# A two-layer hybrid attention trunk on one core: the memory's keys and values become the first chunk of weights, and bank reads of norms and values move ahead of weight work

## The chip, the cores and the metric

The kernel runs on one core of a Trainium2 chip. The metric is the time of one execution in device microseconds (us), median over runs. The engines are TensorE (PE: matmuls and transposes, which write to the banks of PSUM), VectorE (DVE), ScalarE (ACT), GpSimd (POOL) and SyncE (SP). Each takes its own instructions in the order in which the program wrote them. SP issues most of the DMAs, POOL some.

## The reference

Two layers on 512 tokens of width 1024. Layer 0 mixes by dilated windows, layer 1 by grouped queries; both also attend, with four heads, to 256 memory tokens. Cut to what the change touches:

```
for i in range(DEPTH):
    h = rmsnorm(x, norm_g[i])
    mem_h = rmsnorm(mem, mem_norm_g[i])
    proj = einsum('bsd,de->bse', h, w_in[i])
    ...
    kv = einsum('bnd,de->bne', mem_h, w_mem_kv[i]).reshape(B, 256, 2, 4, 128)
    k = rmsnorm(kv[:, :, 0], mem_kn_g[i])
    v = kv[:, :, 1]
    ...
    x = x + einsum('bse,ed->bsd', y * silu(gate), w_out[i])
```

All is float32. The keys and values of the memory don't depend on x, so they may be worked out before or after the first projection of the layer.

## The kernel before

**Precision.** Each float32 operand is split in a high part (a rounded copy, made on ACT) and a low part (what is left, made on DVE), and a product is three matmuls: high x high, high x low, low x high (`mm3`, L162 to L165). Of weights these parts are the tiles `wh` (ACT, L285) and `wo` (DVE, L295); of x the tiles `h`, `hS` (turned by PE at L471, copied by ACT at L157, low part by DVE at L160), of the memory `act`.

**Chunks.** The weights lie in DRAM as pieces of 128x1024 (512 KB), in the order of `PLAN`; the work on them is cut into chunks. A chunk of kind `W2` or `W1` (`s_chunk`, L352) multiplies two 2x2 block matrices with seven products in place of eight, in which sums of weight blocks (`T1` to `T4`) and sums of x blocks (`S1` to `S4`, made from `xs` at L506 to L516) stand for blocks. A chunk of kind `T2`, `T2b` or `O1` (`chunk`, L331) is a plain product. The first three chunks of before are one `W2` (the values of head group 0, from x; 14 pieces of 12 matmuls), and two `T2` (the memory's keys and values; 4 pieces each, again 12 matmuls a piece, `mem_kv` at L593). After them comes the memory's queries, a `W1` chunk.

**What sets the order.** Nothing is scheduled by a planner: the order of an engine's instructions is that in which the Python code emits them. `Driver` keeps generators with due times, counted in slots; a slot is one piece of a `W` chunk or one group of a `T2` chunk. After a group's matmuls come, in this order: `drv.free()` (generators given to `release`, which read banks), `W.advance()` (low parts, weight sums, casts, loads), and `drv.tick()` (generators given to `spawn`). `W.advance` casts a piece ahead of its use, into a ring of four `wh`/`wo` buffers (`RING`, L24); a cast whose buffer is still read waits on its engine and holds what is behind it. `KEEP` (L38) limits how many loaded pieces are held per kind.

**The start.** The gain of the layer's norm is spread over the partitions by one-row matmuls into two banks (`row_bank`, L557); two rows of dummy matmuls (`busy`, L884) keep PE at work. Two of four x tiles are normed (`norm_1`: squares on ACT, the root on POOL; `norm_2`: DVE) and turned, then the first `W2` product begins, while `prep` (L857) norms the other two, makes the sums and turns them. The memory's norm (`mem_norm(0)`) is spawned five slots later, and its keys and values follow after the `W2` chunk. Layer 1 uses the same `mem_kv` and `chunk`, with its first part (`mem_norm(1)`) spawned in layer 0's output projection.

**The evacuations.** `chunk` spawns what follows a bank two slots after its last group, so behind the weight work of that slot. `ev_k` (L597) squares the keys per head, multiplies by the root, turns them, and splits them into `kmT`; `ev_v` (L606) splits the values into `vm`.

Of the kernel before, what the change touches and what calls it, by code (L numbers as in the profile page):

```python
# [24 lines left out]
XW, BOTH = (1, 2, 0, 5), False  # L25
BULK, ACTIVE, MEM_AT, SET_AT, WARM, MEM_B, PREP_Y, ACC_AT, PREP_B, HALF, SET_B = 2, 2, 5, 15, 1, 12, 1, 4, 1, {"a": 3, "b": 3, "o": 0}, 3
MEM_STEP = 1, 1
MEM_D = 4
PD, W_EARLY = 1, True
# [95 lines left out]
def trunk_kernel(ctx: ExitStack, tc: tile.TileContext, x, mem, wall, norm_g, mem_norm_g, gcol,  # L125
# [50 lines left out]

    class Weights:
        def __init__(self):
            self.items, self.last, self.need, self.allocs, self.sums = [], [], [], [], []
            self.users = {}  # L180
            d = g = 0
            for c, kind in enumerate(PLAN):
# [12 lines left out]
                else:  # L195
                    n = 1 if kind in ("W1", "W1b") else 2
                    at = {k: d + i * n for i, k in enumerate(("21", "11", "12", "22"))}
                    d += 4 * n
# [11 lines left out]
            assert d == wall.shape[0], (d, wall.shape)  # L210
# [27 lines left out]
        def sum(self, force=False, want=None):  # L238

            for n, (key, d) in enumerate(self.sums[:8]):  # L240
# [12 lines left out]
                elif k == "T2":  # L253
                    if not (self.ripe(self.load_at, key, force) and self.ripe(self.at, (c, "T1", x), force, 1 if c < T1_DMA else None)):
                        continue
                    if c:
                        G.dma_start(self.tile[key], self.tile[c, "T1", x], accum_op=ALU.add)
                    else:
                        V.tensor_tensor(self.tile[key], self.tile[key], self.tile[c, "T1", x], ALU.add)
# [16 lines left out]
        def hi(self, force=False):  # L276
            i = self.n_hi
            if i >= len(self.items) or not self.ripe(self.at, self.items[i], force, 1 if self.items[i][1] == "T1" and self.items[i][0] < T1_DMA or self.items[i][:2] == (0, "T2") else None):
                return False
# [51 lines left out]
    def chunk(units, nb, group, evac):  # L331

        ps = [None] * nb
        for u in range(units):
# [150 lines left out]
    def proj_t(act, sels, evac):  # L485
# [5 lines left out]
        chunk(2, len(sels), group, evac)  # L491
# [65 lines left out]
    def row_bank(name, times=1):  # L557

        r = [at("row") for _ in range(2)]
# [33 lines left out]
    def mem_kv(layer, M):  # L593
# [249 lines left out]
    for c, n in enumerate(XW):  # L843
        nc.sync.dma_start(xt[c], xv[c])
        W.dma(n)
# [670 lines left out]
```

## Time and profile before

| | |
|---|---|
| median of 3 runs | 972.06 us (971.13 to 972.48) |
| the profiled execution | 971.6 us |
| its span, first to last instruction | 969.8 us |
| PE busy | 949.5 us |
| DVE busy | 793.1 us |
| ACT busy | 675.4 us |
| first weight matmul starts | 9.65 us |
| query chunk starts (after the first three chunks) | 86.32 us |
| mean granted TensorE clock | 1.000 |

The profile is of one execution. Its timeline gives each instruction's start and duration in us, the engine, the line, the operation, and output and inputs by the program's names with the buffer numbers left out; in brackets stands the idle time before it and what ended it. "x8" merges eight equal instructions that follow each other. A view of waits lists who waited for whom, with the total in us, the number of waits and the longest. A view of stretches gives each engine's busy time between two points of the span, with the granted clock, the share of DMA and its GB/s. Instructions overlap their predecessor's drain, so the distance between two starts is shorter than a duration.

### The profile page before, as it was taken

The page shows a single profiled execution, that of the slowest core. Times are in us where ns is not written, and L with a number is a line of the kernel's source. Part 1 is how long each engine was busy: PE and PEld are TensorE (multiplying, and loading weights), DVE is VectorE, ACT ScalarE, POOL GpSimd, SP SyncE. Part 2 cuts the span into 40 slices and gives each one's busy share as a digit, 9 for nine tenths or more (in the row PEclk, how much of TensorE's full clock was granted, in tenths as well). Part 3 has the DMA queues.
Part 4 walks back from the last instruction along what each step waited for, and adds up shares of the span by engine and source line. Part 5 has one row for each costly group of instructions (what it writes and reads, how often), then busy time and mean ns, then how long its engine had stood idle before and what let it go on. Part 6 is the DMA issues. An engine that isn't in the chain of part 4 may idle for free. (4 is left out here: it accounts for less than half of the span.)

```text
span 969.8 us, 16665 instructions
## 1 busy us (share of the span) xinstructions
PE 949.5 (98%) x5728; PEld 835.8 (86%) x5728; DVE 793.1 (82%) x1413; ACT 675.4 (70%) x1687; POOL 332.7 (34%) x480
## 2 busy tenths in 40 slices
PE   8899999999999999999999999999999999999998
PEld 5689988888888888888899996787999999998776
DVE  6997776888888888888898999769888997779863
ACT  6555689686868686868685667545778887878760
POOL 1122423556454545454736011323233231011011
PEclk9999999999999999999999999999999999999999
DMA  8979846968787868685959889959986696786644
GB/s 331 326 267 336 220 102 170 293 131 259 150 256 154 256 153 261 154 260 131 279 134 233 259 203 272 299 191 351 240 178 148 178 241 166 218 213 163 183 140 130
DMA packets 88982, 209.27 MB, mean 216 GB/s; under 512 B 25281, under 2 KB 36033, under 8 KB 88898
## 3 DMA queue, kind: packets, MB, share of 16 engines
q1 hardware_dynamic: 70034, 146.28, 43.5%
q0 software_dynamic: 17568, 59.78, 32.5%
q10 hardware_dynamic: 1296, 2.16, 0.6%
q8 instruction: 45, 0.74, 0.3%
q14 instruction: 39, 0.32, 0.1%
HBM read 157.79 MB, written 12.65 MB: 176 GB/s over the span
## 5 line engine op out<-in xcount | busy, mean ns | idle before, releaser
L295 DVE TENSOR_TENSOR wo<-wl,wh 128x1024 fp32r<-128x1024 f32 x255 | 314.6, 1237 | 12.3 <-ACT wh L285 11.5
L285 ACT CAST wh<-wl 128x1024 fp32r<-128x1024 f32 x255 | 269.7, 1059 | 75.7 <-PE pj L165 39.8
L163 PE MATMUL pj<-wh,hS 128*128 128x512 f32 (+1 forms) x448 | 164.3, 367 | 0.0
L164 PE MATMUL pj<-wo,hS 128*128 128x512 f32 (+1 forms) x448 | 158.1, 353 | 2.6 <-DVE wo L295 2.6
L165 PE MATMUL pj<-wh,hS 128*128 128x512 f32 (+1 forms) x448 | 158.2, 353 | 0.0
L163 PE MATMUL pj<-wh,h 128*128 128x512 f32 (+1 forms) x336 | 123.4, 367 | 0.0
L164 PE MATMUL pj<-wo,h 128*128 128x512 f32 (+1 forms) x336 | 118.8, 354 | 2.3 <-DVE wo L295 2.3
L165 PE MATMUL pj<-wh,h 128*128 128x512 f32 (+1 forms) x336 | 118.9, 354 | 0.0
L420 POOL TENSOR_TENSOR rstd<-mse,half 128x4 f32<-128x4 f32 (+2 forms) x98 | 100.1, 1021 | 8.2
L164 PEld LDWEIGHTS pj<-wo,hS 128*128 128x128 f32 x448 | 85.0, 190 | 13.4 <-DVE wo L295 3.5
L165 PEld LDWEIGHTS pj<-wh,hS 128*128 128x128 f32 x448 | 84.7, 189 | 12.4 <-DVE hS L160 0.3
L163 PEld LDWEIGHTS pj<-wh,hS 128*128 128x128 f32 x448 | 84.8, 189 | 9.7
L419 POOL TENSOR_SCALAR mse<-hss 128x4 f32<-128x4 f32 (+1 forms) x86 | 44.3, 515 | 129.9 <-ACT junk L529 126.1
L360 ACT COPY sn<-pj 128x512 f32<-128x512 f32 x132 | 73.6, 591 | 14.3 <-PE pj L165 10.7
L529 ACT ACTIVATE junk<-sn 128x128 f32<-128x128 f32 x264 | 79.0, 308 | 0.2 <-DVE sn L371 0.2
L987 POOL TENSOR_TENSOR ta<-sn,tabs 128x128 f32<-128x128 f32 (+1 forms) x64 | 37.2, 584 | 119.7 <-DVE sn L534 91.6
L164 PEld LDWEIGHTS pj<-wo,h 128*128 128x128 f32 x336 | 64.0, 190 | 10.0 <-DVE wo L295 2.8
L165 PEld LDWEIGHTS pj<-wh,h 128*128 128x128 f32 x336 | 63.7, 190 | 9.3 <-DVE h L160 0.2
L163 PEld LDWEIGHTS pj<-wh,h 128*128 128x128 f32 x336 | 63.9, 190 | 7.3 <-ACT h L157 0.2
L377 DVE TENSOR_TENSOR sn<-pj,sn 128x512 f32<-128x512 f32 x99 | 67.5, 683 | 3.0 <-PE pj L165 2.6
L269 POOL DMA_DIRECT2D wl<-wl x33 | 29.3, 886 | 112.4 <-DVE wo L295 70.7
L163 PE MATMUL pj<-hS,wh 128*128 128x256 f32 x192 | 55.9, 291 | 0.0
(229 smaller groups left out, 2457.1 us busy)
## 6 DMA issues: line engine op xcount, KB each, us to landing
wl<-in_wall_dram SPq DMA_DIRECT2D x222, 512.0 KB, 6.9
wl<-wl POOLq DMA_DIRECT2D x64, 512.0 KB, 5.8
wl<-in_wall_dram POOLq DMA_DIRECT2D x42, 512.0 KB, 8.5
acc<-sn POOLq DMA_DIRECT2D x16, 256.0 KB, 5.0
od<-o SPq DMA_DIRECT2D x12, 256.0 KB, 5.2
og<-od SPq DMA_DIRECT2D x12, 256.0 KB, 6.8
odb<-o SPq DMA_DIRECT2D x12, 256.0 KB, 2.7
og<-odb SPq DMA_DIRECT2D x12, 256.0 KB, 3.9
```

The source lines that it names most:

```text
L163: T.matmul(o, lh, rh, start=start, stop=False, skip_group_check=True)
L164: T.matmul(o, lh, rl, start=False, stop=False, skip_group_check=True)
L165: T.matmul(o, ll, rh, start=False, stop=stop, skip_group_check=True)
L269: G.dma_start(self.tile[key], self.tile[c, "T2", x], accum_op=ALU.add)
L285: A.copy(wh, self.tile[self.items[i]])
L295: V.tensor_tensor(wo, self.tile[key], wh.bitcast(F32), ALU.subtract)
L360: A.copy(t, b)
L377: V.tensor_tensor(t, b, t, ALU.subtract if q == "12" else ALU.add)
L419: G.tensor_scalar(e, ss, EPS, None, ALU.add)
L420: G.tensor_tensor(r, e, half[:, 0:n], ALU.pow)
L529: A.activation(jk, p[:, j * 128:(j + 1) * 128], AF.Square, scale=QS, accum_out=ss[:, j:j + 1])
L987: G.tensor_tensor(ta[:, 0:n], xn[:, 0:n, 0:32], ropeA[:, 0, b, s0:s0 + n], ALU.mult)
```

## The change

The order of the first chunks is no longer that of `PLAN` (in which the weights still lie in DRAM) but `SEQ`: the two `T2` chunks first, then the `W2`. So the memory tiles and the gain of their norm are loaded and normed ahead of x; the gain of x goes by banks to an SBUF tile (`gain`, copied by ACT in `ahead`); the four x tiles are loaded and normed behind them in `prep`, the x parts turned while the memory's chunk runs. `ahead` turns the memory's tiles just ahead of the groups that use them. The T2 sums of the first `W2` chunk go by DMA. The mask and rope tables are loaded in `setup`. In `chunk`, used by both layers and by the output projections, the evacuation goes to `release` and stands ahead of `W.advance`; `ev_k` gives what follows its squares to `release`, too, and `ev_v` makes its low part at once.

```diff
-KEEP = {"T2": 6, "T2b": 4, "O1": 4, "W1": 9, "W2": 10, "W2s": 9, "W1b": 7, "W2b": 9}
+SEQ = [1, 2, 0] + list(range(3, len(PLAN)))
+KEEP = {"T2": 8, "T2b": 4, "O1": 4, "W1": 9, "W2": 10, "W2s": 9, "W1b": 7, "W2b": 9}
...
-            for c, kind in enumerate(PLAN):
+            for c in SEQ:
+                kind, d = PLAN[c], sum(pieces(k) for k in PLAN[:c])
...
-                    if c:
-                        G.dma_start(self.tile[key], self.tile[c, "T1", x], accum_op=ALU.add)
-                    else:
-                        V.tensor_tensor(self.tile[key], self.tile[key], self.tile[c, "T1", x], ALU.add)
+                    G.dma_start(self.tile[key], self.tile[c, "T1", x], accum_op=ALU.add)
...
+                if pre:
+                    pre(u, b)
                 group(w, u, b, ps[b])
                 drv.free()
+                if u == units - 1:
+                    drv.release(evac(b, ps[b]), 2)
                 W.advance()
-                if u == units - 1:
-                    drv.spawn(evac(b, ps[b]), 2)
                 drv.tick()
...
         def ev_k(b, p):
             r = head_sq(p)
-            yield 2
-            xn = head_mul(p, r)
-            yield 2
-            q = transpose4(xn)
...
+            def rest():
+                xn = head_mul(p, r)
+                yield 2
+                q = transpose4(xn)
+                cs = slice(b * 128, (b + 1) * 128)
+                yield from put_norm(q, gk_m[layer], kt_[0][:, :, cs], kt_[1][:, :, cs])
+            drv.release(rest(), 2)
+            yield 1
...
             A.activation(vt_[0][:, b], p, AF.Copy, scale=0.5)
-            yield 1
             V.scalar_tensor_tensor(vt_[1][:, b], p, 0.5, vt_[0][:, b].bitcast(F32), ALU.mult, ALU.subtract)
+            yield 1
...
-    nc.sync.dma_start(row0, norm_g[0:1, :])
-    rows["x0"] = halves(row0)
-    for c, n in enumerate(XW):
-        nc.sync.dma_start(xt[c], xv[c])
-        W.dma(n)
+    nc.sync.dma_start(row0, mem_norm_g[0:1, :])
+    rows["m0"] = halves(row0)
+    row1 = m4(name="row1")[0:1, :]
+    nc.sync.dma_start(row1, norm_g[0:1, :])
+    rows["x0"] = halves(row1)
+    for b in range(2):
+        nc.sync.dma_start(mt[b], mem[b * 128:(b + 1) * 128])
+        W.dma(1)
+    W.dma(2)
...
+    for c in range(4):
+        nc.sync.dma_start(xt[c], xv[c])
+        if c % 2:
+            W.dma(2)
...
+        for c in range(5):
+            if c < 4:
+                n[c] = norm_1(xb[c])
+            if c:
+                norm_2(xb[c - 1], n[c - 1], rows["x"])
+                if c > 2:
+                    s1.append(sum_h(xb[c - 1]))
+            if 1 < c < 4:
+                put_h(H, "12", c - 2, xb[c - 2][1])
+                put_h(H, "11", c - 2, xb[c - 2][0])
             yield 1
         for c in range(2):
             sums_h(H, xb[c], xb[2 + c], c, s1[c], sums)
-            yield 1
+            yield 2 - c
...
-    first = row_bank("x0", WARM)
+    first = row_bank("m0", WARM)
+    gain = row_bank("x0", 1, pj)
...
-    busy(512)
-    nst[0] = norm_1(xb[0], True)
+    nst = [norm_1(mb[0], True)]
     W.hi(True)
-    norm_2(xb[0], nst[0], first, (1,))
+    norm_2(mb[0], nst[0], first, (0,))
...
+    def ahead(u, b):
+        if (u, b) == (0, 1):
+            for j in range(2):
+                A.copy(rows["x"][j], gain[j])
+            norm_3(mb[1], M, 128, 0)
+            for c in range(2):
+                norm_2(mb[c], nst[c], first, (1,))
+        if (u, b) == (1, 0):
+            for c in range(2):
+                norm_3(mb[c], M, 128 * c, 1)
...
-    drv.spawn(mem_norm(0), MEM_AT)
-    s_chunk(512, H, ev_v0, pre=second)
-    km, vm = mem_kv(0, Ms[0])
+    km, vm = mem_kv(0, M, ahead)
+    s_chunk(512, H, ev_v0)
```

Three places show how the order of instructions moves. The first is ACT's queue at the point where x is first turned (`sq` are the squares of a norm, `junk` those of a key's heads, `h` is x turned, `act` the memory turned). Before, the casts of `h` stand between the first two weight pieces:

```order
L458 ACTIVATE sq,ss<-x 128x512 x2
L157 CAST h_134<-xT 128x4x128
L285 CAST wh<-wl 128x1024
L157 CAST h_134<-xT 128x4x128
L157 CAST h_179<-xT 128x4x128
```

With the change, after the second 24 matmuls of the key chunk:

```order
L462 ACTIVATE sq,ss<-x 128x512 x2
L533 ACTIVATE junk,hss<-pj 128x128 x4
L287 CAST wh<-wl 128x1024 x2
L462 ACTIVATE sq,ss<-x 128x512 x2
L158 CAST h_341<-xT 128x4x128
L158 CAST h_349<-xT 128x4x128
```

The first casts of x now stand behind the seventh and eighth weight pieces (`x2`) and behind the squares of the third x tile.

The second place is DVE's queue around the x sums of the `W2` chunk. Before (`xs_257` to `xs_314`, the second x half's sums; L251 and L259 are weight sums):

```order
L506 TENSOR_TENSOR xs_257<-x 128x512
L295 TENSOR_TENSOR wo<-wl,wh 128x1024
L251 TENSOR_TENSOR wl<-wl 128x1024
L160 TENSOR_TENSOR hS_286<-xT,hS_286 128x4x128
L514 TENSOR_TENSOR xs_284<-xs_235,x 128x512
L515 TENSOR_TENSOR x<-x 128x512
L516 TENSOR_TENSOR xs_285<-x,xs_284 128x512
L295 TENSOR_TENSOR wo<-wl,wh 128x1024
L259 TENSOR_TENSOR wl<-wl 128x1024
L160 TENSOR_TENSOR hS_286<-xT,hS_286 128x4x128
L514 TENSOR_TENSOR xs_314<-xs_257,x 128x512
```

With the change (`xs_446` takes the place of `xs_257`, `xs_534` that of `xs_314`):

```order
L510 TENSOR_TENSOR xs_446<-x 128x512
L297 TENSOR_TENSOR wo<-wl,wh 128x1024 x2
L161 TENSOR_TENSOR hS_465<-xT,hS_465 128x4x128
L518 TENSOR_TENSOR xs_463<-xs_406,x 128x512
L519 TENSOR_TENSOR x<-x 128x512
L520 TENSOR_TENSOR xs_464<-x,xs_463 128x512
L617 SCALAR_TENSOR_TENSOR vm<-pj,vm 128x512
L594 SCALAR_TENSOR_TENSOR kmT<-qT,gc,kmT 128x4x128
L617 SCALAR_TENSOR_TENSOR vm<-pj,vm 128x512
L297 TENSOR_TENSOR wo<-wl,wh 128x1024 x2
L594 SCALAR_TENSOR_TENSOR kmT<-qT,gc,kmT 128x4x128
L161 TENSOR_TENSOR hS_465<-xT,hS_465 128x4x128
```

The row that follows is `xs_534`. The values (`vm`), the keys (`kmT`) and two more weight pieces stand ahead of it. PE turns it right after the second `W2` piece.

The third place is DVE's queue at the start of layer 1, where the same `mem_kv` runs (`tabs` are its rope tables, `xn` is a key's norm, reading the bank `pj`). Before:

```order
L1225 TENSOR_TENSOR tabs<-tbraw,grB 128x512
L534 TENSOR_TENSOR xn<-pj,rstd 128x512
L295 TENSOR_TENSOR wo<-wl,wh 128x1024 x2
L160 TENSOR_TENSOR hS_8035<-xT,hS_8035 128x4x128
L514 TENSOR_TENSOR xs_8066<-xs_7998,acc 128x512
```

With the change:

```order
L1248 TENSOR_TENSOR tabs<-tbraw,grB 128x512
L538 TENSOR_TENSOR xn<-pj,rstd 128x512
L297 TENSOR_TENSOR wo<-wl,wh 128x1024 x2
L1248 TENSOR_TENSOR tabs<-tbraw,grB 128x512
L510 TENSOR_TENSOR xs_8019<-acc 128x512
L538 TENSOR_TENSOR xn<-pj,rstd 128x512
L161 TENSOR_TENSOR hS_8044<-xT,hS_8044 128x4x128
```

Both key norms are now done before the first S1 low part (`hS`), a pair of weight pieces sooner than before.

More of the change, by code (lines that the diff above doesn't have):

```diff
@@ L209, in __init__ @@
                             g += 1
-            assert d == wall.shape[0], (d, wall.shape)
+            assert sum(pieces(k) for k in PLAN) == wall.shape[0]
             self.g = -1
@@ L555, in row_load, with row_bank @@
         rows[name] = halves(t)
-    def row_bank(name, times=1):
-        r = [at("row") for _ in range(2)]
+    def row_bank(name, times=1, bank=at):
+        r = [bank("row") for _ in range(2)]
         for j in (1, 0):
@@ L838, in trunk_kernel @@
     rows = {}
+    mt = [m4(name="m") for _ in range(2)]
     nc.scalar.dma_start(ident, ident_d)
     row0 = m4(name="row0")[0:1, :]
[L841 to L845 removed]
+    nc.sync.dma_start(row0, mem_norm_g[0:1, :])
[7 more added lines that the diff above has]
+    W.dma(2)
     tabA = s2(name="tabA")[:, 0:256].rearrange("p (b c d) -> p b c d", b=2, c=4)
@@ L880, in setup @@
             yield 1
-    first = row_bank("x0", WARM)
+    first = row_bank("m0", WARM)
+    gain = row_bank("x0", 1, pj)
+    rows["x"] = halves(m4(name="row"))
     def busy(n):
-        T.matmul(at("busy")[:, 0:n], ones, rows["x0"][0][0:1, 0:n], start=True, stop=True)
-    busy(512)
-    nst[0] = norm_1(xb[0], True)
+        T.matmul(at("busy")[:, 0:n], ones, rows["m0"][0][0:1, 0:n], start=True, stop=True)
+    mb, M = [halves(t) for t in mt], Act(NM)
+    nst = [norm_1(mb[0], True)]
     W.hi(True)
-    norm_2(xb[0], nst[0], first, (1,))
+    norm_2(mb[0], nst[0], first, (0,))
     def mid():
```

63 lines of the change are left out of this document (23 added, 40 removed).

## The prediction

> **What bounds the kernel now.** I read the page's busy shares first, then the waits of TensorE (PE), then the busy time in stretches, to see which stage has room for the change.
>
> ```profile
> PE 949.5 (98%) x5728; PEld 835.8 (86%) x5728; DVE 793.1 (82%) x1413; ACT 675.4 (70%) x1687; POOL 332.7 (34%) x480
> ...
> PE pj L164 <- DVE wo L295: 6.7, 8, 2.0
> ...
> PE pj L164 <- DVE wo L295: 4.6, 4, 2.0
> PE xT L471 <- DVE h L160: 0.8, 1, 0.8
> ...
> 10.00:16.00 6.00, 5.18 (x21) 4.13 (x21) 4.30 (x7) 3.07 (x8) 0.40 (x2) 1.00 1.02 410
> 16.00:46.00 30.00, 25.42 (x129) 20.25 (x127) 28.53 (x36) 16.95 (x27) 6.01 (x10) 1.00 0.99 317
> 46.00:72.00 26.00, 26.00 (x126) 21.73 (x125) 23.88 (x32) 16.42 (x27) 5.19 (x9) 1.00 0.76 277
> 72.00:110.00 38.00, 38.00 (x255) 35.08 (x254) 26.55 (x26) 22.63 (x54) 12.46 (x15) 1.00 0.95 290
> ```
>
> PE is busy 98% of the span, so the whole is set by matmul work, and no matmul of weight is added or removed. Over the run PE waits 6.7 us for low parts of weights (`wo`, made on VectorE, DVE); the second row of that name is the first 50 us alone: 4.6 of the 6.7. In the stretches (columns PE, PEld, DVE, ACT, POOL) DVE is busy 28.5 of 30 us from 16 to 46 while PE is not full; from 46 on PE is full. So the only place to win or lose more than a microsecond is the first 46 us, and there DVE ends last. The question is whether the new order has DVE ready earlier or later than PE needs it.
>
> **The start of PE.** These rows of the timeline give start, duration, engine and line.
>
> ```profile
> 2.24 3.75 PE L562 MATMUL row<-row,ones 1*128 1x512 f32 x4 [2.24 <-DMA row<-in_norm_g_dram]
> 5.78 1.91 PE L886 MATMUL busy<-row,ones 1*128 1x512 f32 x2
> 7.87 1.11 PE L471 MATMUL xT<-ident,x 128*128 128x128 f32 x4 [0.17 <-DVE x L465]
> 9.02 0.58 ACT L157 CAST h<-xT 128x512 fp32r<-128x512 f32 x1
> 9.65 0.80 PE L163 MATMUL pj<-wh,h 128*128 128x512 f32 x1
> ...
> 10.68 0.63 PE L165 MATMUL pj<-wh,h 128*128 128x512 f32 x1
> 11.10 0.63 PE L163 MATMUL pj<-wh,h 128*128 128x512 f32 x1
> ...
> 15.57 0.39 PE L164 MATMUL pj<-wo,h 128*128 128x512 f32 x1
> 15.80 0.39 PE L165 MATMUL pj<-wh,h 128*128 128x512 f32 x1
> ```
>
> Three one-row products (two `row`, one `busy`) keep PE until 7.69; each costs 1.7 us plus 0.2 of drain (1.91). The change has four, since the gain of x gets banks too and `busy(512)` goes: PE is free for the first transposes at about 7.69 + 1.7 - 0.2 = 9.2. The norm of the first memory tile, some 0.4 us later than that of x now because one more row is loaded ahead of it, is done by 8.2 and not the last. From transposes to the first matmul it takes 9.65 - 7.87 = 1.78, so that matmul starts at 11.0: 1.3 us later than now.
>
> Matmuls step by 0.42 us at 11.10 and by 0.23 at 15.57: PE is at half speed until somewhere before 15.57. The granted-clock column says 1.00 throughout, so I go by the steps. I assume full speed from 15.0 here too: (15.0 - 11.0)/0.42 = 9.5 slow matmuls and 2.5 at 0.23 end the first twelve at 15.6. Bounds: full speed from 13 saves 0.9; from 18 it costs 1.5.
>
> [...]
>
> **Sizes.** The next rows are from the timeline of before, PE, ACT and DVE apart.
>
> ```profile
> 83.70 0.39 PE L165 MATMUL pj<-wh,act 128*128 128x512 f32 x1
> ...
> 85.74 0.39 PE L165 MATMUL pj<-wh,act 128*128 128x512 f32 x1
> 85.97 0.60 PE L541 MATMUL qT<-ident,xn 128*128 128x128 f32 x4
> 86.32 0.36 PE L163 MATMUL pj<-wh,h 128*128 128x256 f32 x1
> ...
> 37.56 1.03 PE L471 MATMUL xT<-ident,xs 128*128 128x128 f32 x8
> 38.20 1.07 ACT L157 CAST hS<-xT 128x512 fp32r<-128x512 f32 x2
> 41.59 1.03 PE L471 MATMUL xT<-ident,x 128*128 128x128 f32 x8
> 45.21 1.03 PE L471 MATMUL xT<-ident,x 128*128 128x128 f32 x8
> ...
> 36.10 2.00 ACT L285 CAST wh<-wl 128x1024 fp32r<-128x1024 f32 x2 [1.97 <-DVE wl L259]
> 17.20 0.63 ACT L458 ACTIVATE sq<-x 128x512 f32<-128x512 f32 x1
> 18.44 1.05 ACT L285 CAST wh<-wl 128x1024 fp32r<-128x1024 f32 x1
> ...
> 662.46 1.41 DVE L465 SCALAR_TENSOR_TENSOR acc<-acc,rstd,row 128x512 f32<-128x512 f32 x2
> 663.78 0.22 DVE L1222 TENSOR_SCALAR grB<-grB 128x128 f32<-128x128 f32 x1
> 665.85 2.35 DVE L295 TENSOR_TENSOR wo<-wl,wh 128x1024 fp32r<-128x1024 f32 x2
> 668.12 0.68 DVE L506 TENSOR_TENSOR xs<-acc 128x512 f32<-128x512 f32 x1
> 668.72 0.68 DVE L1225 TENSOR_TENSOR tabs<-tbraw,grB 128x512 f32<-128x512 f32 x1
> 680.47 0.74 DVE L590 SCALAR_TENSOR_TENSOR kmT<-qT,gc,kmT 128x512 fp32r<-128x512 f32 x1
> 681.13 1.27 DVE L160 TENSOR_TENSOR hS<-xT,hS 128x512 fp32r<-128x512 f32 x2
> ```
>
> Starts are what counts where DVE runs without a break: a 512-wide operation 0.60 (668.12 to 668.72), a pair of norms 1.32 (662.46 to 663.78), two low parts 2.27 (665.85 to 668.12; a weight sum has the same shape), a key's low part 0.66. A warm matmul is 2.04/9 = 0.227 (83.70 to 85.74, ten rows), twelve 2.72; twelve with eight transposes 3.62 (41.59 to 45.21), so four transposes 0.45. A cast follows its transposes' start by 0.64 (37.56 to 38.20) and takes 0.55.
>
> **The key chunk.** After the first twelve the second memory tile is turned and used at once: 15.6 + 0.64 + 0.55 = 16.8, its low part (0.6) by 17.45, the third matmul then, ten more matmuls 2.27: 19.7. The two second halves are turned next: cast by 20.9, but DVE has a pair of norms and two low parts first (17.4 + 1.32 + 2.27 = 21.0), so the low part is there at 21.65; ten matmuls give 24.0, twelve more 26.7. That ends 48 matmuls. Now comes the in-order wait I rest most on. ACT's casts of weight pieces 7 and 8 need ring buffers that PE reads until 26.7, and behind them on ACT stand the squares of x tile 2 and the casts of the first turned x: 26.85 + 1.95 + 1.24 (17.20 to 18.44) + 0.55 = 30.6. DVE, done with the norm of x tile 1 at about 27.2, waits 3.4 us for those casts, because the x low parts stand ahead of its weights.
>
> **The vector engine's run.** From 30.6 to the sum `xs_534` DVE has, without a break, four low parts of turned x, two key norms, two first sums, two S1 low parts, four later sums and two values' low parts (16 x 0.60 = 9.6), two key low parts (1.3), six weight low parts and two weight sums (8 x 1.135 = 9.1), two pairs of norms (2.6): 22.7, ending at 53.3. PE's own work up to that sum, counted from 26.7, is six groups of twelve matmuls and nine blocks of four transposes: 26.7 + 6 x 2.72 + 9 x 0.45 = 47.1. DVE is 6.2 us behind that, and PE meets it in three places. `xs_406`, the first sum, is 7.1 us into the run: 37.7 against 36.7, a wait of 1.0. The low part of the first `W2` piece follows 6.0 later: 43.7 against 42.0, a wait of 1.7. And `xs_534` comes at 53.3 against 49.8, since two later weights, the values and a key stand ahead of it: 3.5. What PE has left then is 12 x 12 matmuls and seven blocks: 12 x 2.72 + 7 x 0.45 = 35.8, so the query chunk begins at 89.1. Now it begins at 86.32 with one block (0.45) still to do, so 86.8 is its like. That is 2.3 us late; six hand-overs between engines at the 0.05 seen from 9.60 to 9.65 add 0.3: **2.6 us**. Behind `xs_534` DVE's load per piece is one low part and two 0.60 operations, 2.3 us against PE's 2.72 to 3.62, so I expect no further wait.
>
> The bounds of this term: by PE's work alone it would be 2.6 - 6.2 = -3.6; if DVE lost another 0.1 us at each of the run's 30 operations, +5.6.
>
> **What costs nothing.** The T2 sums of the first wide chunk leave DVE (2.27 us) for two DMAs on POOL's queue:
>
> ```profile
> wl<-wl POOLq DMA_DIRECT2D x2, 512.0 KB, 7.8
> ...
> 657.65 1.42 DVE L465 SCALAR_TENSOR_TENSOR acc<-acc,rstd,row 128x512 f32<-128x512 f32 x2 [1.45 <-DMA x1d<-acc]
> ...
> PE qT L541 <- DVE xn L534: 0.3, 1, 0.3
> ```
>
> They can start once the second T1 sum is there, at about 41, and land 7.8 us later; PE wants the pieces past 65, so they are hidden. Without that cover the 7.8 us would show. On POOL's queue the two table products of the set-up now stand between these DMAs and the last T4 sums, in the query chunk instead of the value chunk; the T4 pieces are wanted some 20 us after their sources, so 0, and a few us if POOL's order held them. The mask, table and gain loads leave SP's queue near 11 us for slot 15, inside the `W2` chunk: five weight loads pass them, and the first head needs them only after the query chunk. The broadcast load of the memory's gain (512 KB) disappears; DMA isn't the bound, so 0. In layer 1 the earlier key norms stand ahead of two low parts (0.6 later), while the 0.3 wait of qT goes and the accumulator sums come a slot earlier, ahead of a norm that waits 1.45 now for a DMA of them: bounds -1.1 to +0.6, taken as 0.
>
> Sum: 971.6 (the profiled execution; span 969.8 and 1.8 around it) + 2.6 = 974.2. The median of the runs shown is 0.5 above that execution: **974.7 us**. Clock and hand-over bounds put the likeliest case's own range at 973 to 978.
>
> **Rivals.** (1) *DVE isn't late*: if the x casts get through ACT before the weights' buffers are free, or the run is shorter, the 6.2 us of waits go and PE's late start alone is left: 974.7 - 6.2 = 968.5. For it: weight sums and T1/T2 work of DVE fall by 2.27 us, and the value chunk has pieces without sums. Against: the queue is in order and the 3.4 us idle stands ahead of everything. It decides when DVE resumes by 24.4 instead of 30.6; halfway there the time is within 0.2%. (2) *A weight piece is late*: the first T1 load is the 19th big transfer; at 410 GB/s (row 10 to 16) 512 KB take 1.28 us, so about 29 us against a need at 34.7. If its tile is freed only after 27, all of DVE's run is later by what the landing passes 34.7; 3 us of it give 977.7. (3) *Half speed until 18*: 1.5 more, 976.2. (4) *The change only swaps stalls*: the 4.6 us of waits that go are worth what the new ones cost, and the late start is made up in the value chunk: 972.1. For it: DVE's total work in these three chunks falls by only 2.3 us; against: nothing in the list above sums to that by itself.
>
> **How the numbers follow.** What can be told from no change is about 0.2%, 1.9 us. The forecast has 0.52: by its own spread a quarter of that falls within 0.2%. Rival 1 has 0.20 (968.5, wholly faster), 2 and 3 together 0.20 (slower), 4 has 0.08 (same). Slower: 0.39 + 0.20 = 0.59, same 0.13 + 0.08 = 0.21, faster 0.20. The range takes in rival 1's time and rival 2's: 968.4 to 979.0, leaving about 0.1 on either side.
>
> **What would show it.** In the profile of the changed kernel: the first weight matmul at 11.0 and not before 10.5; the first x casts on ACT behind the squares near 30; a DVE wait of some 3 us ahead of the first `h`; PE waits on `xs` and `wo` that sum to about 6 us before 56, the longest ahead of the transposes of `xs` that follow the second `W2` piece; full PE after that; the query chunk at 89. It is wrong if DVE's wait for the `h` casts is under 1 us, if PE waits less than 3 us between 30 and 56, or if the layer 1 start moves by over 1 us.

## The result, and the profile after

The changed kernel takes 977.64 us (median of 6 runs, 974.0 to 978.68), the kernel before beside it 971.6 us (6 runs, 970.47 to 973.47): a ratio of 1.0054, 95% interval 1.0040 to 1.0067. (The ratios given here come from the single runs and not from the medians, whose quotient is 1.0062.) The forecast of slower was right, and 977.64 lies in the range, but the loss is 6.0 us where 2.6 were worked out. The profiled execution is the slowest of the six (978.68, span 976.9), so its 7.1 us over the span of before is about 1 us more than the medians differ.

| | before | forecast | after |
|---|---|---|---|
| first weight matmul | 9.65 | 11.0 | 11.13 |
| end of the key chunk's 48 matmuls | | 26.7 | 27.36 |
| DVE resumes with the low parts of x | | 30.6 | 30.34 |
| `xs_534` (second S2 sum) is done on DVE | | 53.3 | 53.24 |
| PE's waits between 30 and 56 (before: 23 to 50) | 4.6 | 6.2 | 5.06 |
| query chunk starts (before: with one block still to do, 0.45) | 86.32 | 89.1 | 92.07 |
| turning of layer 1's first memory tile | 629.22 | +2.6 | 634.59 |
| turning of layer 1's accumulator | 685.51 | +2.6 | 692.23 |
| span | 969.8 | 972.4 | 976.9 |

First the line of busy times on the page of the changed kernel, and then PE's waits in the first 92 us (total us, number, longest).

```profile
PE 953.8 (98%) x5730; PEld 838.5 (86%) x5730; DVE 790.2 (81%) x1411; ACT 676.2 (69%) x1689; POOL 341.3 (35%) x482
```

```profile
PE xT L475 <- DVE xs L518: 3.2, 1, 3.2
PE row L566 <- DMA row<-in_mem_norm_g_dram: 2.3, 1, 2.3
PE pj L165 <- DVE wo L297: 1.5, 1, 1.5
PE pj L164 <- ACT act L158: 0.9, 2, 0.7
PE xT L475 <- DVE xs L510: 0.4, 1, 0.4
```

The first, third and fifth row are the three waits of the forecast: `xs` of the first sum (0.4 for 1.0), the low part of the first `W2` piece (1.5 for 1.7), and `xs` of the second S2 sum (3.2 for 3.5). They stand in place of 5.4 us of waits of before (4.6 on `wo`, 0.8 on `h`). But PE's busy time has grown by 4.3 us (949.5 to 953.8), with no matmul of weight added. One more one-row product at the start accounts for 1.7 of them; the rest is the sign of matmuls that ran slower. Where they did is in PE's timeline around the longest wait; the brackets hold the wait ahead of an instruction.

```profile
49.67 0.60 PE L475 MATMUL xT<-ident,xs 128*128 128x128 f32 x4
53.46 1.08 PE L475 MATMUL xT<-ident,xs 128*128 128x128 f32 x4 [3.19 <-DVE xs L518]
54.20 0.78 PE L164 MATMUL pj<-wh,h 128*128 128x512 f32 x1
54.77 0.63 PE L165 MATMUL pj<-wo,h 128*128 128x512 f32 x1
...
59.04 0.59 PE L166 MATMUL pj<-wh,h 128*128 128x512 f32 x1
59.47 1.04 PE L475 MATMUL xT<-ident,xs 128*128 128x128 f32 x8
```

After 3.19 us without work the four transposes take 1.08 where 0.60 is usual, and eleven matmuls from 54.77 to 59.47 step by 0.43, the step of the kernel's first microseconds. From 53.46 to 59.47 are 6.01 us, for work that takes 0.45 + 2.72 = 3.17 at full speed: 2.84 us lost behind the wait, nearly as much as the wait itself. The stretches show it in the granted clock, the third figure from the right (ahead of DMA share and GB/s).

```profile
50.00:54.00 4.00, 0.81 (x6) 0.60 (x5) 4.00 (x7) 0.59 (x1) 2.69 (x3) 0.83 1.08 230
54.00:59.00 5.00, 5.00 (x14) 3.98 (x13) 2.94 (x4) 2.51 (x4) 0.00 (x0) 0.50 1.06 210
59.00:61.00 2.00, 2.00 (x13) 1.67 (x12) 0.27 (x1) 0.89 (x2) 0.00 (x0) 0.88 0.59 115
60.00:72.00 12.00, 12.00 (x65) 10.19 (x64) 9.48 (x12) 8.04 (x12) 0.00 (x0) 1.00 0.37 106
```

Missing from full clock are 4 x 0.17 + 5 x 0.50 + 2 x 0.12 = 3.4 us. At half clock that is 6.8 us, begun while PE still waited: in stretches of 1 us the clock is 1.00 up to 52, 0.82 from 52 to 53 and 0.50 from 53. It fell at about 52.6, so 2.4 us after the last transposes had ended (49.67 + 0.60). In stretches of 0.2 us it is 0.59 from 52.6, 0.50 from 52.8 to 59.4, 0.84 from 59.4 and 1.00 from 59.6, which is the 6.8 us again. In before no stretch of 5 us is under 1.00 but at the end (0.94 from 965 to 970); in the changed kernel only these are, and the end (0.87 from 975).

The second place that the sum had not counted is the start of layer 1. PE's timeline there comes first, DVE's second.

```profile
671.45 0.48 PE L164 MATMUL pj<-wh,act 128*128 128x512 f32 x1
673.02 0.50 PE L165 MATMUL pj<-wo,act 128*128 128x512 f32 x1 [1.09 <-DVE wo L297]
...
686.71 0.60 PE L475 MATMUL xT<-ident,xs 128*128 128x128 f32 x4
688.86 0.66 PE L475 MATMUL xT<-ident,xs 128*128 128x128 f32 x4 [1.56 <-DVE kmT L594]
```

```profile
684.10 0.74 DVE L594 SCALAR_TENSOR_TENSOR kmT<-qT,gc,kmT 128x512 fp32r<-128x512 f32 x1
685.18 0.69 DVE L617 SCALAR_TENSOR_TENSOR vm<-pj,vm 128x512 fp32r<-128x512 f32 x1 [0.34 <-ACT vm L616]
685.79 2.36 DVE L297 TENSOR_TENSOR wo<-wl,wh 128x1024 fp32r<-128x1024 f32 x2
688.06 0.75 DVE L594 SCALAR_TENSOR_TENSOR kmT<-qT,gc,kmT 128x512 fp32r<-128x512 f32 x1
```

The second block of keys is turned earlier now, its bank is held until its low part is made, and that `kmT` stands on DVE behind two low parts of weights (2.27 us from start to start) and a value's. PE's next transposes need the bank and wait 1.56 us. Here before had waits of 0.51 and 0.29 on `wo` and 0.35 on `xn`, 1.15 us in all, against 1.09 + 1.56 = 2.65.

So the 7.1 us between the two spans are: 5.3 up to the query chunk (92.07 against 86.77), 1.35 in layer 1 (692.23 - 634.59 = 57.64 against 56.29), and some 0.4 elsewhere.

### The profile page after: what moved, and what is told of

Same layout as the page of the kernel before. It is cut to its first block, busy times and chain, and to the rows that moved or that the text cites. A ratio compares the mean times of both kernels' runs of the same rounds, so it can differ in the third digit from the quotient of the medians.

```text
span 976.9 us, 16687 instructions
## 1 busy us (share of the span) xinstructions
PE 953.8 (98%) x5730; PEld 838.5 (86%) x5730; DVE 790.2 (81%) x1411; ACT 676.2 (69%) x1689; POOL 341.3 (35%) x482
## 5 line engine op out<-in xcount | busy, mean ns | idle before, releaser
L424 POOL TENSOR_TENSOR rstd<-mse,half 128x4 f32<-128x4 f32 (+2 forms) x98 | 103.6, 1057 | 8.2
```

The costliest lines, as they stand in the source:

```text
L424: G.tensor_tensor(r, e, half[:, 0:n], ALU.pow)
```

## The experiments

The changed kernel's theory after this result: (a) 2.5 to 2.8 us are half clock that the wait of 3.2 us brings on; (b) 1.35 us are the new evacuation in layer 1; (c) the rest is VectorE's delay, as forecast. The rivals: the half clock comes by itself at this place or in this run, the wait only covers a VectorE that would be late anyway, and an earlier start would pay in full. All edits but one are of the changed kernel; `e3_evac_only` edits the kernel before. All compute the whole of the reference, and only `e5_fill` does work besides.

The mean granted clock of each execution is known, too. In the profiles of the changed kernel and its variants 1.70 to 1.75 us of clock are missing at six places ahead of the last 20 us, and 3.4 to 3.45 us at two: spells of about 3.4 us at half clock, or of twice that. A short one is 0.0017 of a span, so a mean under 0.999 is taken here as the sign of one or more, though it doesn't tell where. The table has the ratio to the kernel before, the runs under 0.999, and from one profile each the wait on the second S2 sum, the wait on `kmT` in layer 1, and the start of the query chunk.

| kernel | ratio (95%) | runs under 0.999 | S2 wait | `kmT` wait | query chunk |
|---|---|---|---|---|---|
| before, three series | 1 | 9 of 27, 6 of 17, 11 of 23 | none | none | 86.77 with its last block |
| changed | 1.0054 (1.0040 to 1.0067) | 5 of 6 | 3.2 | 1.6 | 92.07 |
| c0_after_again | 1.0056 (1.0037 to 1.0075) | 6 of 6 | 3.2 | 1.5 | 91.35 |
| e1_sums_slot | 1.0025 (1.0010 to 1.0039) | 4 of 12 | none | 2.6 | 87.25 |
| e5_fill | 1.0038 (1.0022 to 1.0055) | 2 of 8 | 0.5 | 1.8 | 89.86 |
| e2_layer1_old | 1.0041 (1.0026 to 1.0056) | 6 of 8 | 3.2 | none | 91.12 |
| e3_evac_only | 1.0024 (1.0013 to 1.0035) | 6 of 12 | none | 1.1 | 86.55 |
| e4_casts_first | 1.0032 (1.0020 to 1.0043) | 12 of 12 | 3.2 | 1.7 | 89.94 |
| e7_gain_dma | 1.0046 (1.0030 to 1.0063) | 6 of 6 | 3.2 | 2.0 | 90.09 |
| e8_two_waits | 0.9979 (0.9966 to 0.9991) | 1 of 12 | none | none | 87.28 |
| e9_no_gain | 0.9979 (0.9966 to 0.9992) | 1 of 12 | none | none | 85.04 |
| e6_all | 0.9951 (0.9933 to 0.9969) | 1 of 6 | none | none | 83.19 |

**c0_after_again.** The changed kernel once more, unedited, to stand beside the second series.

> The changed kernel itself, beside the others on the same chip. With the clock falling or not behind the 3.2 us wait, its runs should spread from about 974 (clock 1.000) to 979 (clock 0.996), median 976 to 978; if its slowness had nothing to do with the clock, the runs would not sort by the clock column.

Measured: 978.66 us (977.23 to 980.7), ratio 1.0056; the three waits are 0.37, 1.50 and 3.17 us. The clock is 0.87 from 50 to 55 and 0.78 from 55 to 60, so 1.75 us are missing where the first profile missed 3.4: 3.5 us at half clock in place of 6.8. The waits of the program are the same to 0.03 us as in the first profile, and what the clock makes of them is not. The median lies above the 976 to 978 that was expected, and no run is at full clock; they do sort by clock, from 977.23 at 0.998 to 980.7 at 0.994, but for one.

**e1_sums_slot.** The S2 sums are turned one slot later; their making on DVE is not moved.

```diff
             sums_h(H, xb[c], xb[2 + c], c, s1[c], sums)
-            yield 2 - c
+            yield 2
```

> The changed kernel with the transposes of the S2 sums one slot later (both x halves yield 2). My theory: the changed kernel loses 3.2 us of waiting at the second S2 sum, and that wait lets the TensorE clock fall to half for the next twelve matmuls (54.2 to 59.6, 5.4 us where 2.7 is usual). With one piece of matmuls between, the wait shrinks to about 0.4 us and the clock stays at 1.0: 5 to 5.5 us less than the changed kernel, about 972 to 973. Rival A, the half clock has nothing to do with the wait: only the wait goes, about 975. Rival B, the late vector engine moves the wait to the low part of the next weight piece: under 1.5 us less, 976 or more.

These are two places in PE's timeline, the S2 transposes and the `kmT` wait of layer 1, and then the stretches around both, with one more, from 880.

```profile
51.05 0.50 PE L165 MATMUL pj<-wo,h 128*128 128x512 f32 x1 [0.30 <-DVE wo L297]
...
53.69 1.06 PE L475 MATMUL xT<-ident,xs 128*128 128x128 f32 x8
...
683.93 0.66 PE L475 MATMUL xT<-ident,xs 128*128 128x128 f32 x4 [2.55 <-DVE kmT L594]
```

```profile
50.00:54.00 4.00, 3.70 (x18) 2.72 (x17) 4.00 (x6) 1.54 (x2) 2.69 (x3) 1.00 1.09 260
54.00:59.00 5.00, 5.00 (x31) 4.25 (x30) 5.00 (x7) 3.01 (x6) 0.00 (x0) 1.00 1.06 211
...
681.00:685.00 4.00, 1.45 (x13) 1.21 (x12) 4.00 (x6) 2.48 (x5) 0.00 (x0) 1.00 1.06 318
685.00:690.00 5.00, 5.00 (x32) 5.00 (x31) 2.99 (x5) 1.73 (x4) 0.00 (x0) 0.66 1.04 282
...
880.00:885.00 5.00, 3.46 (x20) 3.26 (x21) 5.00 (x10) 3.85 (x9) 0.68 (x1) 0.83 0.18 34
```

The transposes of both halves now stand behind the next twelve matmuls. DVE is as late as it was (its second S2 sum starts at 53.30, 0.66 later still), and PE doesn't wait for it: all eight transposes go in one block at 53.69. The clock stays at 1.00, though the DMAs are as busy as in the changed kernel (shares of 1.09 and 1.06, there 1.08 and 1.06), so busy DMAs are not what lowers it. The query chunk starts 4.8 us earlier than in the changed kernel (87.25 against 92.07). The ratios show only 2.8 us of it (1.0054 to 1.0025), the medians 4.2, and the median of 974.11 lies between the time of the clock theory and that of rival A, so the time alone doesn't decide between them; the profile does. It also shows where some of the rest goes: it is the slowest of the 12 runs, and it loses its clock twice further on, 1.70 us of it each time: behind the `kmT` wait in layer 1, which has grown to 2.55 us, and at 883 us, after waits of PE of 0.3 and 1.5 us for `pbT` (0.83 from 880 to 885, and again from 885 to 890). The runs fall in two groups: 8 at 0.999 or above, median 973.19, and 4 below, median 977.60; of these four only the profiled one tells where.

**e5_fill.** DVE is as late as in the changed kernel, but PE turns the identity 24 times into a spare bank ahead of the second S2 transposes.

```diff
+                if fill and i == 0 and c:
+                    f = at("busy")
+                    for _ in range(fill):
+                        T.transpose(f[:, 0:128], ident, ident)
                 put_h(H, k, c, sums[c][i])
```

> The changed kernel with 24 extra transposes of the identity (128x128, into a spare bank) ahead of the second half's S2 transposes, where TensorE waits 3.2 us; nothing else moves. My theory: the wait itself stays as covered time, but the clock doesn't fall: the twelve matmuls behind take 2.7 us in place of 5.4, 2.7 us less than the changed kernel, about 975. Rival A, the slow matmuls have another cause (the DMA queue at over 100% share in the same stretch, or the weights): no gain, 977 to 978, or slower by the transposes' own time.

These are PE's rows at that place; the matmuls between the third and fourth row go at full step.

```profile
50.26 0.60 PE L475 MATMUL xT<-ident,xs 128*128 128x128 f32 x4
50.69 2.78 PE L529 MATMUL busy<-ident 128*128 128x128 f32 x24
54.02 0.63 PE L475 MATMUL xT<-ident,xs 128*128 128x128 f32 x4 [0.55 <-DVE xs L518]
...
57.26 0.93 PE L475 MATMUL xT<-ident,xs 128*128 128x128 f32 x7
```

The sum comes no earlier (the transposes start at 54.02), and yet the work behind them takes 57.26 - 54.02 = 3.24 us where the changed kernel took 6.01. Dummy work in the wait keeps the clock (1.00 from 50 to 60), so the idle time is the cause and not the place, nor the DMAs, whose share from 54 to 59 is 1.07 here. The query chunk starts 2.2 us earlier, and only 2 of 8 runs are under 0.999. The ratio fell by 0.0016, some 1.6 us; the two intervals overlap, so the gain in time isn't shown by itself.

**e2_layer1_old.** The old place of the evacuation in layer 1 and in the output projections; the first chunks keep the new one (the diff is cut to its core).

```diff
-                if u == units - 1:
+                if u == units - 1 and not old:
                     drv.release(evac(b, ps[b]), 2)
                 W.advance()
+                if u == units - 1 and old:
+                    drv.spawn(evac(b, ps[b]), 2)
...
-            drv.release(rest(), 2)
-            yield 1
+            if layer:
+                yield 2
+                yield from rest()
+            else:
+                drv.release(rest(), 2)
+                yield 1
```

> The changed kernel with the evacuation of before in layer 1 alone: the keys and values of its memory and the rest of the output projections spawn behind the weight work, as before; layer 0 keeps the change. My theory: the 1.4 us that layer 1's start loses between 629 and 692 us of the changed kernel (waits on wo of 1.1 and on kmT of 1.6 against 0.5, 0.3 and 0.3) come back: 1 to 1.7 us less, about 976.2. Rival: the loss there is of the half clock's making or of weights that come late, and stays: 977.6.

PE's waits in layer 1 are now 0.69 and 0.30 on `wo` and 0.34 on `xn`, and the stretch from the memory tile's turning to the accumulator's takes 56.54 us, that of before being 56.29. The S2 wait stays at 3.17 with one spell of 3.4 us at half clock (0.85 from 50 to 55, 0.81 from 55 to 60). So the 1.35 us of layer 1 are the evacuation's, by the profile. The ratio falls by 0.0013, which fits, but its interval overlaps that of the changed kernel.

**e3_evac_only.** The same term from the other side: the kernel before with the new evacuation alone (`release` ahead of `W.advance`, `rest` given to `release`, the value's low part at once).

> The kernel before with the new evacuation alone (release ahead of the weight work in the plain chunks, the rest of the key norm by release, the values' low part at once); the order of the chunks is that of before. My theory: layer 0's memory chunk has slack there and doesn't move, layer 1's start loses 1.0 to 1.5 us: 0.1 to 0.15% slower than before. Rival: read banks early is the useful half of the change, and it is 0.1% or more faster.

PE's rows with a wait in layer 1:

```profile
665.92 0.50 PE L164 MATMUL pj<-wo,act 128*128 128x512 f32 x1 [1.19 <-DVE wo L295]
...
681.33 0.66 PE L471 MATMUL xT<-ident,xs 128*128 128x128 f32 x4 [1.12 <-DVE kmT L590]
```

Both new waits are there without the new order of chunks; the stretch takes 57.37 us (1.08 more than in before), and the whole kernel 1.0024 of before, where 1.0010 to 1.0015 was expected. So this part of the change does harm in layer 1 by itself. The profiled run is the fastest of the 12 (971.79), with a span within 0.1 us of before's, so it doesn't show where the whole loss arises.

**e4_casts_first.** In `prep` the squares of the next x tile are given out behind the casts of the turned x, and not ahead of them. This is the in-order wait on which the prediction rested most.

```diff
-            if c < 4:
-                n[c] = norm_1(xb[c])
             if c:
                 norm_2(xb[c - 1], n[c - 1], rows["x"])
...
                 put_h(H, "11", c - 2, xb[c - 2][0])
+            if c < 4:
+                n[c] = norm_1(xb[c])
```

> The changed kernel with the squares of an x tile behind the casts of the turned x in ACT's queue, in place of ahead of them. My theory: VectorE's run starts when the first cast of turned x is done; without the 1.24 us of squares it starts at 29.1 in place of 30.3, and TensorE's three waits (0.4, 1.5, 3.2) shrink by 1.2 in all; with 2 us left of the long wait the clock falls less often: 1.2 to 3 us less than the changed kernel, 975 to 976.5. Rival A, VectorE's later work, not its start, sets the waits: no gain. Rival B, the roots of x tiles 2 and 3 come too late behind the squares: the wait moves to a norm, 0 or a loss.

DVE's rows ahead of the first low parts of x, of the changed kernel and then of this one:

```profile
27.40 1.41 DVE L469 SCALAR_TENSOR_TENSOR x<-x,rstd,row 128x512 f32<-128x512 f32 x2 [1.04 <-POOL rstd L424]
30.34 1.29 DVE L161 TENSOR_TENSOR h<-xT,h 128x512 fp32r<-128x512 f32 x2 [1.52 <-ACT h L158]
```

```profile
27.64 1.41 DVE L469 SCALAR_TENSOR_TENSOR x<-x,rstd,row 128x512 f32<-128x512 f32 x2 [1.04 <-POOL rstd L424]
29.36 1.29 DVE L161 TENSOR_TENSOR h<-xT,h 128x512 fp32r<-128x512 f32 x2 [0.30 <-ACT h L158]
```

The wait for ACT falls from 1.52 to 0.30 us, as expected. DVE resumes 1.0 us earlier than in the first profile and 1.5 earlier than in c0_after_again (30.89). PE's waits go from 5.04 (0.37 + 1.50 + 3.17 in c0_after_again) to 4.06, and its second S2 transposes start 1.52 earlier (52.49 against 54.01): VectorE's delay does set PE's. What was expected and did not come is a shorter long wait: the first two took all of the gain, the S2 wait stays at 3.17, one spell of 3.4 us at half clock stays in the profile (0.80 from 50 to 55, 0.86 from 55 to 60), and all 12 runs are under 0.999. The ratio falls by 0.0024 against the same series, 2.3 us.

**e7_gain_dma.** The gain of x comes by a broadcast DMA of 512 KB, as the memory's gain did in before, and no longer by one-row products and two copies: 2 us less of PE's start.

```diff
-    row1 = m4(name="row1")[0:1, :]
-    nc.sync.dma_start(row1, norm_g[0:1, :])
-    rows["x0"] = halves(row1)
...
+    row_load("x", norm_g[0:1, :])
...
-    gain = row_bank("x0", 1, pj)
-    rows["x"] = halves(m4(name="row"))
...
-            for j in range(2):
-                A.copy(rows["x"][j], gain[j])
```

> The changed kernel with the gain of x spread over the partitions by one DMA of 512 KB (as the memory's gain was before) in place of two one-row products and two copies on ACT. My theory: the first transposes start when the memory's norm is done, at 8.2 in place of 9.3, so all of the start is 1.1 us sooner: 0.7 to 1.3 us less than the changed kernel, about 976.5. Rival: the half-speed phase lasts to the same point in time whatever starts first, and about half of it is lost again: 0.3 to 0.6 less.

Two views again: the start on PE with the `kmT` wait of layer 1, and the stretches behind the S2 wait and behind that one.

```profile
7.46 1.11 PE L475 MATMUL xT<-ident,m 128*128 128x128 f32 x4 [1.29 <-DVE m L469]
8.51 0.79 PE L908 MATMUL busy<-row,ones 1*128 1x128 f32 x2
9.25 0.79 PE L164 MATMUL pj<-wh,act 128*128 128x512 f32 x1
...
685.45 1.09 PE L475 MATMUL xT<-ident,xs 128*128 128x128 f32 x4 [2.00 <-DVE kmT L594]
```

```profile
50.00:55.00 5.00, 3.49 (x11) 2.94 (x12) 4.92 (x8) 2.37 (x4) 0.70 (x1) 0.56 1.07 212
55.00:60.00 5.00, 5.00 (x23) 4.05 (x22) 1.32 (x4) 2.01 (x4) 0.00 (x0) 0.75 0.69 137
...
685.00:690.00 5.00, 4.55 (x26) 4.56 (x27) 4.61 (x7) 1.53 (x2) 0.00 (x0) 0.66 1.05 273
```

The first transposes start at 7.46, earlier than the 8.2 expected, and the first matmul comes at 9.25, 1.97 us earlier than in c0_after_again, and the S2 wait is 3.18 us as ever. The transposes behind it start 2.50 us earlier (51.51 against 54.01), so the half speed of the start took nothing back. But 5 x 0.44 + 5 x 0.25 = 3.45 us of clock are missing behind the wait, where c0_after_again missed 1.75. The query chunk starts only 1.26 us earlier. In layer 1 another 5 x 0.34 = 1.7 us are missing, behind a `kmT` wait of 2.00 us that has grown by 0.5. The ratio falls by 0.0010; over the six runs the mean clock is 0.9955, that of c0_after_again 0.9965, so about 1 us more of clock went.

**e8_two_waits.** `e1_sums_slot` and `e2_layer1_old` together: both places of a long wait gone.

> The changed kernel with two edits that were tried apart: the S2 sums a slot later (as in e1_sums_slot, which measured 1.0025 of the kernel before) and the old evacuation in layer 1 and the output projections (as in e2_layer1_old, 1.0041). The changed kernel itself measured 1.0054 and 1.0056. If the two waits only add, the ratio is 1.0055 - 0.0030 - 0.0014 = 1.0011, 1.1 us over the kernel before. If the lost clock makes up part of the time, and is lost behind whichever long wait is left (half of the runs of e1_sums_slot lost it in layer 1, where this edit takes the wait away), both together gain more than their sum: the mean granted clock is 0.999 to 1.000 in nearly all runs, the ratio 0.9995 to 1.0005, and the runs lie closer together than the 6.8 us of e1_sums_slot. The first theory expects the runs as far apart as there.

Measured: 971.87 us (969.31 to 973.18), ratio 0.9979, where adding the two gains gave 1.0011. The runs lie 3.9 us apart and 1 of 12 is under 0.999, as the clock theory said. Its ratio is lower still than that theory's 0.9995 to 1.0005, and part of that is the kernel before: in this series 11 of its 23 runs lost clock. Its 12 others have a median of 972.29, and the 11 of e8_two_waits at full clock 971.82: a ratio of 0.9995. That correction doesn't hold in general: in the first series of before the 9 runs under 0.999 (median 972.23) were as fast as the 18 others (972.42).

**e9_no_gain.** All the edits of `e6_all` but the gain's: `e8_two_waits` and `e4_casts_first`.

> e6_all (0.9951 of the kernel before) without its gain edit: the gain of x is spread by one-row products again, so the first matmul comes at 11.1 instead of 9.5. In e7_gain_dma this edit alone brought 1.0 us of the 1.9 us by which the first matmul came earlier. If what was missing there was given back to the clock behind the 3.2 us wait, which is gone here, then the whole 1.6 to 1.9 us shows: a ratio of 0.9968 to 0.9971. If the early start is worth only 1.0 us for another reason (VectorE sets the pace from 30 us on), the ratio is 0.9961, and the query chunk starts at 84.2 instead of 84.8 to 85.1.

Measured: 971.25 us (969.66 to 972.43), ratio 0.9979, above the figures of both theories; the interval takes in that of the clock theory (0.9968 to 0.9971) and not the other's 0.9961. `e6_all` is 0.0028 lower, 2.7 us, so the gain's edit seems to have its whole worth once the S2 wait is gone; the query chunk starts at 85.04, as the clock theory said, and 1.85 later than in `e6_all`. The interval of that difference (0.6 to 4.9 us, the two intervals' half-widths added in squares) doesn't shut out 1.0 us, but the start of the query chunk isn't the 84.2 of the other theory. Another miss is the comparison with e8_two_waits: the query chunk comes 2.24 us earlier, and the median only 0.6 us.

**e6_all.** The edits of e1, e2, e4 and e7 together.

> All repairs in one: the changed order of chunks with the S2 transposes a slot later, the casts of x ahead of the squares, the gain of x by DMA, and layer 1's evacuation as before. My theory: no wait over 1.5 us is left ahead of 60 us and the clock stays, so what the new order saves shows: against the changed kernel without a clock loss (974.0) less 2.9 (S2) less 1.2 (squares) less 1.1 (start) less 1.3 (layer 1): 967 to 969, faster than before by 0.3% or more. Rival, the new order itself is the loss (DVE has too much ahead of the x sums whatever the slots): 971 to 973, like before.

Measured: 968.94 us (966.93 to 971.02) against 973.3 of the kernel before, ratio 0.9951, faster than both. The longest wait of PE from the first weight matmul to the query chunk is 0.9 us. PE's early waits once the gain's first row has landed, by total, count and longest:

```profile
PE xT L477 <- DVE m L471: 1.3, 1, 1.3
PE pj L165 <- DVE wo L297: 1.2, 2, 0.9
PE pj L164 <- ACT act L158: 0.9, 2, 0.7
```

The gains one by one are 0.0029, 0.0024, 0.0010 and 0.0013 of the time, 0.0076 in all; together they bring 0.0105. The intervals of the single gains, added in squares, are wider than that difference, so the times don't show that the gains are more than additive. The start of the query chunk points that way, from one profile each and beside c0_after_again: 4.10 + 1.41 + 1.26 = 6.77 us earlier by e1, e4 and e7, and 8.16 by e6_all.

## Why the prediction was right, and where its size was off

**Right: the start.** The first matmul at 11.13 (11.0 forecast), full step from 15.12 (15.0), twelve matmuls done at 15.82 (15.6). That shuts out rival 3, half speed until 18. These rows are PE's of the changed kernel.

```profile
2.25 7.16 PE L566 MATMUL row<-row,ones 1*128 1x512 f32 x8 [2.25 <-DMA row<-in_mem_norm_g_dram]
9.34 1.12 PE L475 MATMUL xT<-ident,m 128*128 128x128 f32 x4
...
11.13 0.80 PE L164 MATMUL pj<-wh,act 128*128 128x512 f32 x1
...
15.12 0.39 PE L164 MATMUL pj<-wh,act 128*128 128x512 f32 x1
```

**Right in its end, off in its parts: the wait of DVE for the turned x.** DVE resumed at 30.34 (30.6). The idle time is 1.04 us ahead of the norm, for POOL's root, and 1.52 ahead of `h`, not 3.4 in one piece: the norm itself came later than I had it. On ACT only the second of the two weight casts waited for PE, and just 0.31 us.

```profile
26.19 1.05 ACT L287 CAST wh<-wl 128x1024 fp32r<-128x1024 f32 x1
27.55 1.05 ACT L287 CAST wh<-wl 128x1024 fp32r<-128x1024 f32 x1 [0.31 <-PE pj L166]
28.50 0.63 ACT L462 ACTIVATE sq<-x 128x512 f32<-128x512 f32 x1
...
29.74 1.05 ACT L158 CAST h<-xT 128x512 fp32r<-128x512 f32 x2
```

The casts at 29.74 stand behind the squares, as forecast, and e4_casts_first showed that this order costs 1.2 us of DVE's waits and 1.0 us of PE's.

**Right: the run of DVE.** 22.9 us from 30.34 to 53.24, where the sum is done and the next operation starts, against 22.7 by counting operations; it met no late transfer, so rival 2 fell, and DVE was late, so rival 1 fell. What is handed to DMAs or moved on POOL cost nothing: PE has no wait from 60 to 72, and waits for no weight sum.

**Right: the three waits of PE,** in place, order and cause; 5.06 us in sum for 6.2, or 5.7 if counted as the forecast did, from start to start (26.10 less the 20.4 of PE's own work). PE met the second S2 sum at 53.46, 26.10 us after the end of the key chunk, for which the forecast had 26.6.

**Mis-sized: PE's work behind `xs_534`.** "What PE has left then is 12 x 12 matmuls and seven blocks ... 35.8" took every matmul at the warm step of 0.227. It took 92.07 - 53.46 = 38.6; the 2.8 us over it are the 2.84 that the four transposes and twelve matmuls lost at half clock. With the 0.66 us by which the key chunk ended late and the 0.5 saved up to the sum, this is the whole distance from 89.1 to 92.07. That the wait brings the half clock on is shown by e5_fill, which fills it, and by e1_sums_slot, which has none. The prediction had the half clock at the start only, and no rival was a wait that costs more than its own length. The forecast's own range of 973 to 978 does hold 977.64, but its width was meant for the clock at the start and for hand-overs; that it covers this term and the next is luck.

**Mis-sized: layer 1.** "Bounds -1.1 to +0.6, taken as 0" measured +1.35. The prediction had the key norms ahead of low parts; what it missed is the other end of `ev_k`, the last low part `kmT`, which now frees a bank that PE waits for while two weights' low parts stand ahead of it. e2_layer1_old and e3_evac_only show it from both sides. The move of layer 1 by over 1 us, which the prediction had named as a sign that it was wrong, came true.

**The sum.** The profiled span is 4.5 us over the forecast's 972.4: 2.7 up to the query chunk (5.3 for 2.6), 1.35 in layer 1, 0.4 elsewhere. The profile is 1.0 over the median of its six, where the forecast had the median 0.5 over the profile; so the median is 2.9 us over: 977.64 for 974.7.

The traces do tell how long the half clock lasts. The profiles of the changed kernel and its variants have eight falls of the clock ahead of the last 20 us. Two of them, in the changed kernel and at e7's S2 wait, began 0.8 to 0.9 us before PE resumed (about 52.6 against 53.46, and 50.6 against 51.51, worked out from the clock missing from 50 to 54), and lasted 6.8 to 6.9 us; the six others began at most 0.4 us before it or after it, and lasted 3.4 to 3.5.

Open: what sets the moment of the fall, and why one of the six runs (974.0 us, clock 1.000) has none behind the same wait; where the runs of the kernel before under 0.999 lose it, since its one profile is at 1.000; why the `kmT` wait, in kernels that don't touch it, was anything from 1.5 to 2.6 us; and why e9_no_gain's 2.2 us in the profile became 0.6 in the median. One of its runs at a mean clock of 0.993 took 971.32, no longer than the rest, so the mean clock of a run isn't its time alone.

## What to carry to other kernels

Price a wait of TensorE of about 2 us or more at its length and, as a risk, up to 2.8 us lost to half clock behind it (falls came here behind waits of 2.00, 2.55 and 3.2 us), and look first for a way to break it up: a block of matmuls between two sums that come late, here one slot, brought the query chunk 4.1 us forward, a start 2 us faster 1.3. When an evacuation is moved forward, follow its last operation, not its first: the bank comes free where that one stands in its engine's queue (here a wait of 1.56 us for `kmT`). An edit that removes one stall can look small while another stall is left, as the earlier start did here, so try the combination before dropping it.

## What the hardware showed that was not expected

A wait of 3.19 us dropped the clock, though the matmuls and four transposes ran up to its start; the prediction had no fall there. A wait of 2.00 us in layer 1 of e7_gain_dma and one of 2.55 us in e1_sums_slot were followed by 3.4 us at half clock each, too (0.66 from 685 to 690 in both). Length alone doesn't decide: the kernel before has a wait of 1.97 us at full clock, and in e1_sums_slot waits of 0.3 and 1.5 us came ahead of a fall. In e1_sums_slot the transposes and matmuls directly behind the wait of 2.55 us still ran at full step, up to 685.4, and then the step went from 0.12 to 0.21 for 128x256.

The kernel before, whose longest wait of PE after its start is 2.0 us, ran under 0.999 in 26 of 67 runs, more often than the three kernels without the S2 and `kmT` waits (3 of 30) and less often than the five with an S2 wait of 3.2 us (35 of 38); the three with a `kmT` wait but no long S2 wait lie between (12 of 32). And 7.2 us of one-row products from 2.25 to 9.41 did not lift the speed of the matmuls at 11.13 to 14.7, which step by 0.43; the granted-clock column reads 1.00 there.
